# Turning the residual by DMA instead of on TensorE in a two-layer transformer trunk

## The chip, the cores and the metric

The kernel runs on one core of one Trainium2 chip. Its time is the device time of one execution in microseconds (us). The engines named below are TensorE (PE in the profile, with PEld for its weight loads), VectorE (DVE), ScalarE (ACT), GpSimd (POOL) and SyncE (SP); SP does no arithmetic, it issues transfers by DMA.

## The reference

What is computed is a decoder trunk of two layers on 256 positions with 2048 channels in float32. Layer 0 mixes with sliding-window attention and an mLSTM (a matrix memory), layer 1 with a "forgetting attention"; both have a SwiGLU feed-forward part of 5632 hidden channels.

```python
h = x                                              # (1, 256, 2048)
for layer in range(2):
    xn = rms_norm(h, norm_mix[layer])
    if layer == 0:
        mix = swa_mlstm_mixer(xn, ...)             # ends in "... @ w_out"
    else:
        mix = forgetting_attention_mixer(xn, ...)  # begins with "xn @ w_in", ends in "out @ w_out"
    h = h + mix
    xn = rms_norm(h, norm_ffn[layer])
    h = h + (silu(xn @ w_gate[layer]) * (xn @ w_up[layer])) @ w_down[layer]
return rms_norm(h, norm_final)
```

## The kernel before

**Products.** Every float32 product is made of three matmuls: operands are split into a high part and a remainder (`hi`, `lo`), and `hi·hi + hi·lo + lo·hi` is summed in PSUM. TensorE needs the left operand with the channel on the partitions, so the kernel keeps the normalised residual turned, as `xh` and `xl`, 16 tiles of 128 channels by 256 positions each. The output of a mixer stands turned in `mh`, `ml`. The 1/rms of each position is applied later, to results; the turned values carry only the norm's gain `gT`.

**Weights.** `load_raw` (L108) loads a chunk of 256 rows and 512 columns, 512 KB, on SP's queue; `split_chunk` (L151) casts it to `hi` on ACT (L154) and subtracts on DVE for `lo` (L155). There are four raw buffers and six pairs of `hi`/`lo`. `gemm` (L168) walks such chunks: 12 matmuls with 512 columns for a chunk (two tiles of channels, two of positions, three matmuls each; L182 to L184).

**Mixed pairs.** Gate and up, the two halves of a down projection, and query and key are multiplied together in `pair_group` (L431). Most pairs of tiles are done plainly (12 matmuls a matrix, L367 to L369); two or three of six or eight are "mixed": a scheme of seven products instead of eight, for which sums of the weights (L462 to L468) and sums of the turned operand are needed (`sums_of`, L217). Which pairs are mixed, and in which order pairs come, is in tables of (kind, pair), with kind 1 for mixed: `ORDER` (L36) for gate and up, `DOWN` (L37) and `DOWN_END` (L41) for the down projections. A group ends with additions on DVE that put the shared products together (L488 to L491) and into `h` (L612, then `add_out`, L259).

**Turning the residual.** `h` stands with positions on the partitions, 128 by 2 by 2048. It is made in blocks of 512 columns, and three times in the kernel all four blocks are finished and have to be turned for what follows: after each layer's output projection (for the FFN) and after layer 0's last down projection (for layer 1). These are the twelve norm blocks. `split_scaled` (L228) does one of them:

```python
pt = pm.tile([P, 2, NT, P], F32, tag="pm", name="pt")
...
nc.tensor.transpose(pt[:, i, t, :], h[:, t, k * P : (k + 1) * P], ident)      # L234
...
nc.scalar.mul(xh[:, k, :], src, g)                                            # L239
nc.vector.scalar_tensor_tensor(out=xl[:, k, :], ...)                          # L240
```

That is eight float32 transposes of 128 by 128 on TensorE for a block, then four products on ACT and four on DVE, and the sums for mixed pairs. In `out_proj` (L351) the output projection is done in two pairs of blocks: both blocks of a pair are multiplied up to the last four tiles of channels, then each one's rest is done and it is added and turned. `close` (L573) calls `add_out` and `split_scaled` at the end of layer 0's last down groups.

**A turn by DMA is in the kernel already.** The FFN's hidden values `c`, also blocks of 512 columns, are turned under the next group's matmuls: two copies on ACT separate the upper and lower 16 bits of each float (L543), four transposing DMAs on SP's queue turn these planes (L545), and two copies on ACT (L550) join them again. The joining is put off by `todo` lists of (position, function): `run_due` (L163) runs a function when `pair_group` reaches that position, behind the latest weight cast. `MID` (6) and `MID_DOWN` (5) are its positions. Twenty blocks are turned this way; the last group before each down projection is turned on TensorE.

**The start of layer 1.** After the FFN, `project` makes the last 272 columns of the input projection first (256 of the values and 16 forget gates, L969), then the gates are worked out on ACT and DVE, while `v_part(0)` makes the first 512 value columns (`first`, L1011 and L1026).

**Order.** Tiles and pools decide who waits for whom; a scheduler orders each engine's instructions when the kernel is built, and `issue_after` keeps an instruction behind another in that order. Each engine then works through its own queue in order.

## Time and profile before

| | us |
|---|---|
| median of three runs | 2113.64 |
| the runs | 2113.04 to 2115.53 |
| the profiled execution | 2115.51 |
| its span in the profile | 2113.8 |
| TensorE busy | 2096.8 (99%) |
| DVE busy | 1823.7 (86%) |
| ACT busy | 1280.7 (61%) |
| granted clock of TensorE, mean | 0.997 |

One execution is profiled, and its rows are in microseconds from the start of the span, or in nanoseconds for a mean duration. A group of instructions is named by line, engine, operation and by output and inputs (`pt<-ident,h`). "DMA to landing" is the time from the issue of a transfer to its last byte. Matmuls overlap: the next begins before the one ahead has ended, so that the cost of one is read from the distance of starts, not from its duration.

### The profile page before, as it was taken

The numbers are of one execution on the slowest core, as the hardware profiler recorded it, in microseconds if no ns is written. First come the engines' busy times: TensorE is split into PE (matmuls) and PEld (weight loads), VectorE is DVE, ScalarE is ACT, GpSimd is POOL, SyncE is SP. The second block draws the span as 40 slices with busy tenths as digits, with TensorE's granted clock in tenths as the row PEclk, the third lists the DMA queues.
The fourth block names the chain that finished last, engine by engine and source line by source line (L and its number), as shares of the span: only waits on it lengthen the run. The fifth ranks groups of instructions, "written<-read, shape, count | busy, mean of one in ns | idle before, by whom it ended". The sixth has DMA issues, their size and how long they took to land.

```text
span 2113.8 us, 26987 instructions
## 1 busy us (share of the span) xinstructions
PE 2096.8 (99%) x9654; PEld 1740.8 (82%) x9654; DVE 1823.7 (86%) x2402; ACT 1280.7 (61%) x1637; POOL 50.6 (2%) x74
## 2 busy tenths in 40 slices
PE   8999999999999999999999999999999999999998
PEld 6878888888888888888888888888888888888886
DVE  6688777899999998999887888778899998998995
ACT  6565555665577646766565546566755677556763
POOL 2100000000000000000000000000000000000000
PEclk9999999999999999999999999999999999999999
DMA  9445666766577666666675655666656667656763
GB/s 316 125 139 181 222 208 182 220 194 204 194 221 221 213 197 212 221 219 189 179 220 172 179 172 166 202 198 203 212 183 220 218 209 205 224 189 209 229 208 131
DMA packets 258998, 423.04 MB, mean 200 GB/s; under 512 B 56576, under 2 KB 64816, under 8 KB 258864
## 3 DMA queue, kind: packets, MB, share of 16 engines
q1 hardware_dynamic: 256976, 415.49, 63.0%
q0 software_dynamic: 1744, 5.81, 1.0%
...
q14 instruction: 59, 0.48, 0.1%
...
HBM read 408.67 MB, written 2.11 MB: 194 GB/s over the span
## 4 chain that ended last, share of the span: by engine, by line
PE 96%; DVE 2%; DMA 1%; issue 0%; ACT 0%; SPq 0%; DVEq 0%; POOLq 0%; POOL 0%; ACTq 0%
PE acc L367 20%; PE acc L368 20%; PE acc L369 20%; PE prod L367 5%; PE prod L368 5%; PE prod L369 5%; PE acc L184 5%; PE acc L183 5%; PE acc L182 5%; PE vacc L182 1%; PE vacc L184 1%; PE vacc L183 1%; DVE lo L155 1%; PE ptm L268 1%; PE po L338 1%
## 5 line engine op out<-in xcount | busy, mean ns | idle before, releaser
L154 ACT CAST hi<-raw 128x1024 fp32r<-128x1024 f32 (+1 forms) x664 | 676.9, 1031 | 486.9 <-PE acc L369 266.1
L155 DVE TENSOR_TENSOR lo<-raw,hi 128x1024 fp32r<-128x1024 f32 (+1 forms) x664 | 788.0, 1200 | 140.1 <-ACT hi L154 138.1
L368 PE MATMUL acc<-lo,xh 128*128 128x512 f32 x1207 | 470.2, 390 | 0.5 <-DVE lo L155 0.5
L367 PE MATMUL acc<-hi,xh 128*128 128x512 f32 x1207 | 466.6, 390 | 0.3 <-DVE u L488 0.2
L369 PE MATMUL acc<-hi,xl 128*128 128x512 f32 x1207 | 464.9, 389 | 0.0
L367 PEld LDWEIGHTS acc<-hi,xh 128*128 128x128 f32 x1207 | 226.6, 188 | 48.3 <-DVE u L488 1.1
L368 PEld LDWEIGHTS acc<-lo,xh 128*128 128x128 f32 x1207 | 226.6, 188 | 47.7 <-DVE lo L155 0.8
L369 PEld LDWEIGHTS acc<-hi,xl 128*128 128x128 f32 x1207 | 226.6, 188 | 47.2
L368 PE MATMUL acc<-lo,mh 128*128 128x512 f32 x444 | 173.1, 390 | 0.0
L369 PE MATMUL acc<-hi,ml 128*128 128x512 f32 x444 | 171.1, 389 | 0.0
L367 PE MATMUL acc<-hi,mh 128*128 128x512 f32 x444 | 170.1, 389 | 0.0
L256 ACT CAST ht<-raw 128x1024 fp32r<-128x1024 f32 x94 | 98.7, 1050 | 53.7 <-issue 19.4
L257 DVE TENSOR_TENSOR lt<-raw,ht 128x1024 fp32r<-128x1024 f32 x94 | 114.8, 1221 | 15.2 <-ACT ht L256 14.9
L182 PE MATMUL acc<-hi,mh 128*128 128x512 f32 x320 | 126.9, 397 | 0.0
L183 PE MATMUL acc<-lo,mh 128*128 128x512 f32 x320 | 125.4, 392 | 0.0
L184 PE MATMUL acc<-hi,ml 128*128 128x512 f32 x320 | 124.8, 393 | 0.0
L256 ACT CAST ht<-t 128x1024 fp32r<-128x1024 f32 x94 | 98.9, 1052 | 41.1 <-PE prod L369 28.3
L257 DVE TENSOR_TENSOR lt<-t,ht 128x1024 fp32r<-128x1024 f32 x94 | 114.6, 1219 | 7.4 <-ACT ht L256 7.4
L256 ACT CAST hi<-raw 128x512 fp32r<-128x512 f32 (+1 forms) x115 | 72.5, 630 | 79.8 <-PE acc L369 68.4
L257 DVE TENSOR_TENSOR lo<-raw,hi 128x512 fp32r<-128x512 f32 (+1 forms) x115 | 80.6, 701 | 24.6 <-ACT hi L256 24.5
L367 PEld LDWEIGHTS acc<-hi,mh 128*128 128x128 f32 x444 | 83.3, 188 | 17.5
L369 PEld LDWEIGHTS acc<-hi,ml 128*128 128x128 f32 x444 | 83.4, 188 | 17.3
...
## 6 DMA issues: line engine op xcount, KB each, us to landing
raw<-in_w_gate_dram SPq DMA_DIRECT2D x176, 512.0 KB, 4.5
raw<-in_w_up_dram SPq DMA_DIRECT2D x176, 512.0 KB, 4.7
raw<-in_w_down_dram SPq DMA_DIRECT2D x176, 512.0 KB, 4.8
raw<-in_w_in_odd_dram SPq DMA_DIRECT2D x88, 512.0 KB, 4.6
raw<-in_w_in_even_dram SPq DMA_DIRECT2D x64, 512.0 KB, 4.6
raw<-in_w_out_even_dram SPq DMA_DIRECT2D x32, 512.0 KB, 4.1
raw<-in_w_out_odd_dram SPq DMA_DIRECT2D x32, 512.0 KB, 4.4
...
```

The costliest lines, as they stand in the source:

```text
L154: latest[0] = nc.scalar.copy(hi[:, :, 0:n], raw[:, :, 0:n])
L155: nc.vector.tensor_tensor(out=lo[:, :, 0:n], in0=raw[:, :, 0:n], in1=hi[:, :, 0:n].bitcast(F32), op=ALU.subtract)
L182: nc.tensor.matmul(o, ah[:, ts], hi, start=(k == 0), stop=False)
L183: nc.tensor.matmul(o, ah[:, ts], lo, start=False, stop=False)
L184: nc.tensor.matmul(o, al[:, ts], hi, start=False, stop=(k == k_all - 1))
L256: nc.scalar.copy(dst_h, src)
L257: nc.vector.tensor_tensor(out=dst_l, in0=src, in1=dst_h.bitcast(F32), op=ALU.subtract)
L268: nc.tensor.transpose(pt[:, i, :], s_, ident)
L338: nc.tensor.matmul(po, v_of(j, 0), t0[:, j, :], start=True, stop=False)
L367: nc.tensor.matmul(o, ah, hi, start=start, stop=False)
L368: nc.tensor.matmul(o, ah, lo, start=False, stop=False)
L369: nc.tensor.matmul(o, al, hi, start=False, stop=stop)
```

## The change

All twelve norm blocks are turned by DMA. `turn_scaled` takes the place of `split_scaled`. It makes two copies on ACT that separate `h` into 16-bit planes and returns two functions: `start` issues four transposing DMAs on SP, and `join` makes two joining copies and the products and sums as before, reading SBUF instead of PSUM. Blocks 1 and 3 (n = 0 and 2) use the tiles of `c` and `tmp` as planes; blocks 2 and 4 (n = 1 and 3) use three buffers of the FFN's ring of raw chunks (`turn_tiles`).

The functions are kept in lists and run between later work. In `out_proj` the first two blocks' functions run between the chunks of blocks 3 and 4 (`run_next`), and for this the second pair of blocks is multiplied singly, first all of block 3, then all of block 4. What is left runs in the first FFN group at the positions `TURN_AT`. For layer 0's last down projection, the functions of blocks 1 and 2 run in the second group at `TURN_DOWN`, those of blocks 3 and 4 in `first_values`, the new start of layer 1: value columns on channel tiles 0 to 7, the 272-wide tail on tiles 0 to 7, then values on tiles 8 to 11, the rest of the values and the rest of the tail. `ORDER` and `DOWN_END` change: for gate and up pair 4 is mixed in place of pair 3, and the pairs now come in the order of their numbers; in `DOWN_END` the mixed pair 4 comes behind the plain pair 5.

```diff
--- before.py
+++ after.py
@@ -33,15 +33,17 @@
 OFF_QM, OFF_KM, OFF_VM, OFF_OM = 1536, 2048, 2560, 3584
 CAP = 15.0
 FILL = 24
-ORDER = ((0, 0), (0, 1), (1, 2), (0, 4), (1, 3), (0, 5), (1, 6), (0, 7))
+ORDER = ((0, 0), (0, 1), (1, 2), (0, 3), (1, 4), (0, 5), (1, 6), (0, 7))
 DOWN = {
     6: ((0, 0), (0, 1), (1, 2), (0, 3), (1, 4), (0, 5)),
     8: ((0, 0), (0, 1), (1, 2), (0, 3), (1, 4), (0, 5), (1, 6), (0, 7)),
 }
-DOWN_END = ((0, 0), (0, 1), (1, 2), (0, 3), (1, 4), (0, 5), (0, 6), (0, 7))
+DOWN_END = ((0, 0), (0, 1), (1, 2), (0, 3), (0, 5), (1, 4), (0, 6), (0, 7))
 QK_ORDER = ((0, 0), (0, 1), (1, 2), (0, 4), (1, 3), (0, 5), (1, 6), (0, 7))
 V_AT = 8
 HEAD_STEPS = ((0, 1), (0, 2), (1, 3), (0, 2), (1, 3), (2,), (3,))
+TURN_AT = (1, 2, 3, 5)
+TURN_DOWN = (2, 3, 4, 6)
 MID = 6
 MID_DOWN = 5
 RAWS = 4
@@ -225,32 +227,45 @@
         nc.vector.tensor_tensor(out=s[:, 3, :], in0=full[:, 1, 0, :], in1=s[:, 1, :], op=ALU.subtract)
         split_plain(sh, sl, s)
 
-    def split_scaled(idx, n, extra=None):
-        for half in range(2):
-            pt = pm.tile([P, 2, NT, P], F32, tag="pm", name="pt")
-            for i in range(2):
-                k = 4 * n + 2 * half + i
-                for t in range(NT):
-                    nc.tensor.transpose(pt[:, i, t, :], h[:, t, k * P : (k + 1) * P], ident)
-            for i in range(2):
-                k = 4 * n + 2 * half + i
-                src = pt[:, i, :, :].rearrange("p t q -> p (t q)")
+    def turn_scaled(room, idx, n, extra=None):
+
+        hu = h[:, :, n * NB : (n + 1) * NB].bitcast(U16).rearrange("p t (n b) -> p t n b", b=2)
+        flat, turned, ct = room.turn_tiles(n % 2)
+        for b in range(2):
+            nc.scalar.copy(flat[:, b, :, :], hu[:, :, :, b])
+
+        def start():
+            with tc.issue_after(load[0].ins):
+                for b in range(2):
+                    for t in range(NT):
+                        nc.sync.dma_start_transpose(turned[b][:, :, t, :], flat[:, b, t, :])
+
+        def join():
+            cb = ct.bitcast(U16).rearrange("p (n b) -> p n b", b=2)
+            for b in range(2):
+                nc.scalar.copy(cb[:, :, b], turned[b].rearrange("p k t q -> p (k t q)"))
+            cols = ct.rearrange("p (k q) -> p k q", k=4)
+            for i in range(4):
+                k = 4 * n + i
                 g = gT[:, idx * KT + k : idx * KT + k + 1]
-                nc.scalar.mul(xh[:, k, :], src, g)
+                nc.scalar.mul(xh[:, k, :], cols[:, i, :], g)
                 nc.vector.scalar_tensor_tensor(
-                    out=xl[:, k, :], in0=src, scalar=g, in1=xh[:, k, :].bitcast(F32), op0=ALU.mult, op1=ALU.subtract
+                    out=xl[:, k, :], in0=cols[:, i, :], scalar=g, in1=xh[:, k, :].bitcast(F32), op0=ALU.mult, op1=ALU.subtract
                 )
-            pair = 2 * n + half
-            if extra is not None and pair in mixed_of(ORDER):
-                sh, sl, pool = extra
-                j = mixed_of(ORDER).index(pair)
-
-                def copies(full):
+            for half in range(2):
+                pair = 2 * n + half
+                if extra is None or pair not in mixed_of(ORDER):
+                    continue
+                m = mixed_of(ORDER).index(pair)
+
+                def copies(full, half=half, pair=pair):
                     for i in range(2):
                         g = gT[:, idx * KT + 2 * pair + i : idx * KT + 2 * pair + i + 1]
-                        nc.scalar.mul(full[:, i, :], pt[:, i, :, :].rearrange("p t q -> p (t q)"), g)
-
-                sums_of(pool, sh[:, j, :, :], sl[:, j, :, :], copies)
+                        nc.scalar.mul(full[:, i, :], cols[:, 2 * half + i, :], g)
+
+                sums_of(room, extra[0][:, m, :, :], extra[1][:, m, :, :], copies)
+
+        return start, join
 
     def split_plain(dst_h, dst_l, src):
         nc.scalar.copy(dst_h, src)
@@ -348,20 +363,32 @@
             ks = slice(k_tile + q, k_tile + q + 2)
             split_plain(mh[:, ks, :], ml[:, ks, :], po)
 
-    def out_proj(w, idx, key, extra, begun=None):
+    def run_next(pending):
+        if pending:
+            with tc.issue_after(latest[0].ins):
+                pending.pop(0)()
+
+    def out_proj(w, idx, key, extra, room, begun=None):
         last = KT - 4
+        pending = []
         for n0 in (0, 2):
             if n0 == 0 and begun:
                 accs = begun
             else:
                 accs = [new_acc() for _ in range(2)]
-                for i in range(2):
-                    gemm(accs[i], m_of, w, (n0 + i) * NB, NB, 0, last, KT)
             for i in range(2):
+                if n0:
+                    for k0 in range(0, last, 4):
+                        gemm(accs[i], m_of, w, (n0 + i) * NB, NB, k0, k0 + 4, KT)
+                        if k0 or i == 0:
+                            run_next(pending)
                 gemm(accs[i], m_of, w, (n0 + i) * NB, NB, last, KT, KT)
                 add_out(accs[i], n0 + i)
-                split_scaled(idx, n0 + i, extra)
+                pending += turn_scaled(room, idx, n0 + i, extra)
                 square_sum(key, n0 + i)
+            if n0 == 0:
+                pending = pending[0::2] + pending[1::2]
+        return pending
 
     def three(o, ah, al, hi, lo, start, stop):
         nc.tensor.matmul(o, ah, hi, start=start, stop=False)
@@ -396,6 +423,23 @@
 
         def tmp(self, shape, name):
             return self.pool.tile(shape, F32, tag="tmp", name=name, bufs=2)
+
+        def turn_tiles(self, odd):
+            shape = [P, 4, NT, P]
+            if odd:
+                a, b, ct = (self.pool.tile([P, 2 * NB], F32, tag="raw", name="turn", bufs=self.raws) for _ in range(3))
+                flat = a.bitcast(U16).rearrange("p (b t n) -> p b t n", b=2, t=NT)
+                turned = [
+                    b.bitcast(U16)[:, i * 2 * NB : (i + 1) * 2 * NB].rearrange("p (k t q) -> p k t q", k=4, t=NT)
+                    for i in range(2)
+                ]
+                return flat, turned, ct
+            c = self.c()
+            flat = (
+                c[:, 2:4, :].bitcast(U16).rearrange("p a n -> p (a n)").rearrange("p (b t n) -> p b t n", b=2, t=NT)
+            )
+            turned = [self.pool.tile(shape, U16, tag="tmp", name="turned", bufs=2) for _ in range(2)]
+            return flat, turned, c[:, 0:2, :].rearrange("p a n -> p (a n)")
 
     class Inside(Room):
 
@@ -491,9 +535,8 @@
         nc.vector.tensor_tensor(out=c[:, 3, :], in0=prods[1], in1=c[:, 1, :], op=ALU.add)
         return plain, c
 
-    def ffn(layer, fp, sx, sd, key, idx_next=None, key_next=None, finish=None):
+    def ffn(layer, fp, room, pending, sx, sd, key, idx_next=None, key_next=None, finish=None, then=None):
         r = rstd(key)
-        room = Room(fp)
 
         def sums_x(pair):
             j = mixed_of(ORDER).index(pair)
@@ -503,7 +546,8 @@
             end = g1 == PARTS[-1]
             nk = 4 * (g1 - g0)
             order = DOWN[nk // 2]
-            todo = []
+            todo = list(zip(TURN_AT, pending))
+            pending = []
             for g in range(g0, g1):
                 par = (g1 - 1 - g) % 2
                 plain, c = pair_group(
@@ -577,7 +621,7 @@
                     finish(acc, n, gf)
                 else:
                     add_out(acc, n)
-                    split_scaled(idx_next, n)
+                    pending.extend(turn_scaled(room, idx_next, n))
                     square_sum(key_next, n)
 
             gf = None
@@ -596,9 +640,10 @@
                     sums_d,
                     [(wd, n0 * NB), (wd, (n0 + 1) * NB)],
                     DOWN_END if end and n0 == 2 else order,
-                    todo,
+                    todo + list(zip(TURN_DOWN, pending[0::2] + pending[1::2])),
                 )
                 todo = []
+                pending = []
                 if end and idx_next is None:
                     gf = [fp.tile([P, CK, NB], F32, tag="raw", name="gf", bufs=RAWS) for _ in range(2)]
                     for i in range(2):
@@ -612,13 +657,16 @@
                         nc.vector.tensor_tensor(out=o, in0=c[:, 2 * m + t, :], in1=o, op=ALU.add)
                 for m in range(2):
                     close(plain[m], n0 + m)
+        if then:
+            then(pending[0::2] + pending[1::2])
 
     def close_layer(layer, w_out, idx, key, begun=None, **rest):
         with tc.tile_pool(name=f"fp{layer}", bufs=2) as fp:
             nd = max(len(mixed_of(o)) for o in DOWN.values())
             sd = [fp.tile([P, nd, 4, P], F32R, name=f"sd{i}", bufs=1) for i in range(2)]
-            out_proj(w_out, idx, key, (*sx, Room(fp)), begun)
-            ffn(layer, fp, sx, sd, key, **rest)
+            room = Room(fp)
+            pending = out_proj(w_out, idx, key, sx, room, begun)
+            ffn(layer, fp, room, pending, sx, sd, key, **rest)
 
 
     def free_halves():
@@ -952,11 +1000,23 @@
 
     late = ctx.enter_context(tc.tile_pool(name="late", bufs=1))
     sx = [late.tile([P, len(mixed_of(ORDER)), 4, P], F32R, name=f"sx{i}") for i in range(2)]
-    close_layer(0, w_out_even[0], 2, "f0", begun=begun0, idx_next=1, key_next="m1")
-
+    wi1 = w_in_odd[0]
+    VT = 2 * FD
+    c_v = 2 * FOX_H * FD
+    vacc0 = [bank(1, "vacc") for _ in range(NT)]
+    tacc1 = new_acc()
+    FIRST_ODD = [(0, 0, NB, k) for k in range(0, 8, 2)] + [(1, 14 * FD, VT + FOX_H, k) for k in range(0, 8, 2)]
+    FIRST_ODD += [(0, 0, NB, k) for k in (8, 10)]
+
+    def first_values(pending):
+        for acc, c0, n, k0 in FIRST_ODD:
+            gemm((vacc0, tacc1)[acc], x_of, wi1, c_v + c0, n, k0, k0 + 2, KT)
+            if (acc, k0) in ((0, 4), (0, 6), (1, 4), (0, 10)):
+                run_next(pending)
+
+    close_layer(0, w_out_even[0], 2, "f0", begun=begun0, idx_next=1, key_next="m1", then=first_values)
 
     r1 = rstd("m1")
-    wi1 = w_in_odd[0]
     with tc.tile_pool(name="od", bufs=1) as od:
         def nat1(acc, n, name, bufs=1):
             t_ = od.tile([P, NT, n], F32, tag=name, name=name, bufs=bufs)
@@ -964,9 +1024,10 @@
                 nc.scalar.mul(t_[:, t, :], acc[t][:, 0:n], r1[:, t : t + 1])
             return t_
 
-        VT = 2 * FD
-        c_v = 2 * FOX_H * FD
-        acc = project(wi1, c_v + 14 * FD, VT + FOX_H)
+        gemm(vacc0, x_of, wi1, c_v, NB, 12, KT, KT)
+        vns = {0: nat1(vacc0, NB, "vn", bufs=2)}
+        acc = tacc1
+        gemm(acc, x_of, wi1, c_v + 14 * FD, VT + FOX_H, 8, KT, KT)
         fg = od.tile([P, NT, FOX_H], F32, name="fg")
         for t in range(NT):
             nc.vector.scalar_tensor_tensor(
@@ -994,8 +1055,6 @@
             j = mixed.index(pair)
             return sx[0][:, j, :, :], sx[1][:, j, :, :]
 
-        vns = {}
-
         def v_part(i):
             vw = NB if i < 3 else VT
             acc = [bank(1, "vacc") for _ in range(NT)]
@@ -1007,8 +1066,6 @@
 
             return part
 
-        first = v_part(0)
-        first(0, 8)
         pc = pm.tile([P, NB], F32, tag="pm", name="pcf")
         nc.tensor.matmul(pc[:, 0:FOX_H], upper, nl[:, 0, :], start=True, stop=True)
         nc.tensor.matmul(pc[:, FOX_H : 2 * FOX_H], ones, nl[:, 0, :], start=True, stop=False)
@@ -1023,7 +1080,6 @@
         nc.vector.tensor_copy(negct, pr[0:FOX_H, 0:S])
         scratch = dp.tile([FOX_H, S], F32, name="scratch")
         nc.gpsimd.dma_start(scratch, negct)
-        first(8, KT)
         for i in range(4):
             qt = od.tile([P, 4, S], F32, tag="qt", name="qtf")
             kt = od.tile([P, 4, S], F32, tag="kt", name="ktf")
```

## The prediction

> **What bounds the kernel now.** I read the page first, then the transposes that the change removes, TensorE's instructions around one of them, and the turns by DMA that the kernel already makes.
>
> ```profile
> span 2113.8 us, 26987 instructions
> PE 2096.8 (99%) x9654; PEld 1740.8 (82%) x9654; DVE 1823.7 (86%) x2402; ACT 1280.7 (61%) x1637; POOL 50.6 (2%) x74
> PE 96%; DVE 2%; DMA 1%; issue 0%; ACT 0%; SPq 0%; DVEq 0%; POOLq 0%; POOL 0%; ACTq 0%
> ```
>
> The third line is the chain that ended last: 96% of the span is TensorE following itself. An instruction taken off TensorE shortens the span by its own slot, as long as whatever replaces it delivers before TensorE asks. DVE at 86% has some slack and ACT at 61% much.
>
> The tile view of `pt`, the PSUM tile of the transposes:
>
> ```profile
> L234 PE MATMUL pt<-ident,h x96: 270/272/273, 296.4 to 1421.6; 128*128 128x128 f32 x96
> L239 ACT ACTIVATE xh<-pt,gT x48: 456/474/502, 300.6 to 1423.0; 128x256 fp32r<-128x256 f32 x48
> L240 DVE SCALAR_TENSOR_TENSOR xl<-pt,gT,xh x48: 474/478/484, 301.1 to 1423.5; 128x256 fp32r<-128x256 f32 x48
> ```
>
> There are 96, eight for each of twelve blocks. Their 272 ns is latency; the slot is read from starts, in TensorE's timeline:
>
> ```profile
> 295.29 0.39 PE L184 MATMUL acc<-hi,ml 128*128 128x512 f32 x1
> ...
> 296.19 0.39 PE L182 MATMUL acc<-hi,mh 128*128 128x512 f32 x1
> 296.42 0.38 PE L234 MATMUL pt<-ident,h 128*128 128x128 f32 x2
> 296.56 0.48 PE L183 MATMUL acc<-lo,mh 128*128 128x512 f32 x1
> 296.87 0.39 PE L184 MATMUL acc<-hi,ml 128*128 128x512 f32 x1
> ...
> 298.03 0.39 PE L183 MATMUL acc<-lo,mh 128*128 128x512 f32 x1
> 298.26 0.82 PE L234 MATMUL pt<-ident,h 128*128 128x128 f32 x6
> 298.83 0.48 PE L182 MATMUL acc<-hi,mh 128*128 128x512 f32 x1
> 299.15 0.40 PE L183 MATMUL acc<-lo,mh 128*128 128x512 f32 x1
> ```
>
> From 295.29 to 296.19 four 512-wide matmuls start, 0.227 us each. From 296.19 to 296.87 lie two of these and two transposes: 0.68 - 0.45 = 0.23. From 298.03 to 299.15, two and six transposes: 1.12 - 0.45 = 0.67. So a transpose costs 0.111 us with its change-over, and a block 0.90 us.
>
> **What goes: 10.7 us.** 12 blocks x 0.90. The products `xh`, `xl` stay in number (48 and 48), read from SBUF instead of PSUM; the same two forms from SBUF at the start of the kernel show whether that costs:
>
> ```profile
> L637 ACT ACTIVATE xh<-xc,gT x16: 492/495/511, 4.2 to 19.1; 128x256 fp32r<-128x256 f32 x16
> L638 DVE SCALAR_TENSOR_TENSOR xl<-xc,gT,xh x16: 477/480/486, 4.8 to 20.0; 128x256 fp32r<-128x256 f32 x16
> ```
>
> DVE 480 against 478, ACT 495 against 474: DVE gets no new work, and its count of instructions stays the same.
>
> **What comes.** Per block: two copies on ACT that separate the 16-bit halves, four transposing DMAs on SP's queue, two copies on ACT that join the halves. The kernel makes 20 such turns of the same size already, under the FFN's matmuls:
>
> ```profile
> L543 ACT COPY c<-c x40: 1037/1043/1047, 393.1 to 2035.6; 128x1024 uint16<-128x1024 uint16 x40
> 394.21 5.25 SPq L545 DMA_TRANSPOSE turned<-c  x4
> DMA to landing us min/median/max: 2.4/2.9/6.3
> L550 ACT COPY c<-turned x40: 1339/1354/1374, 406.7 to 2043.8; 128x1024 uint16<-128x1024 uint16 x40
>   DMA turned<-c: 6.4, 5
> ```
>
> ACT pays 2 x 1.04 + 2 x 1.35 = 4.8 us a block, 57 us in twelve, beside 833 us in which it is idle. SP is held 5.25 us by four issues; no weight load leaves it then. From the first copy to the last landing: 2.1 + 3 x 1.31 + 2.9 = 8.9 us, and 2.7 for the joining. The last row says that ACT waited for such landings five times in forty, 6.4 us in all. Whether stages bear it is read from windows (length, then busy time and count on PE, PEld, DVE, ACT and POOL, granted clock, DMA share, GB/s):
>
> ```profile
> 393.00:402.00 9.00, 9.00 (x42) 7.44 (x41) 7.01 (x7) 7.61 (x9) 0.00 (x0) 1.00 0.88 197
> ...
> 296.40:346.00 49.60, 49.60 (x232) 41.20 (x231) 34.07 (x48) 29.35 (x50) 0.00 (x0) 1.00 0.63 183
> 346.00:388.00 42.00, 42.00 (x191) 34.76 (x190) 37.78 (x51) 26.60 (x32) 0.69 (x1) 1.00 0.65 201
> 985.00:1027.00 42.00, 42.00 (x195) 34.78 (x194) 34.88 (x47) 24.22 (x38) 0.00 (x0) 1.00 0.43 130
> 1027.00:1045.00 18.00, 17.47 (x116) 15.88 (x115) 16.66 (x35) 11.28 (x23) 0.69 (x1) 1.00 0.65 206
> ```
>
> The first row holds a turn of today, with TensorE busy throughout. The others are the stages that get turns: the end of the first out-projection, the first FFN group, the last down group of layer 0, the start of layer 1. ACT is idle 20.2, 15.4, 17.8 and 6.7 us there and needs at most 4 x 4.8 = 19.2 over the first two. DVE is the fuller engine (37.78 of 42) and is not charged. The DMA share leaves room.
>
> **Where cover is thin.** I walked the queues in the order in which the changed kernel's instructions are built, with a matmul at 0.227 us and the durations above, and compared when each turned block can be there with when TensorE asks. ACT's queue is the one to watch: casts of weights stand behind each joining copy, which waits for its landing. SP is second: loads stand behind transposes that wait for ACT.
>
> Blocks 1 and 2 of an out-projection (edits: split in start and join, run between chunks) are needed one full block pair later, 2 x 96 x 0.227 = 43.6 us; free. Block 3, finished 21.8 us earlier than its pair mate now that the two run singly, is joined before the FFN starts; the single run itself costs nothing, since no weight is shared between blocks. Block 4 ends with the FFN's start: h added and split 3 us in, four issues until 8, landed by 11, joined and multiplied by 16 (the DMA row's median; 2.7 + 4 x 0.47). Behind it on ACT stands the last cast of the first mixed pair, done by 17; TensorE's 82nd matmul asks for it at 82 x 0.227 = 18.6. Its own pairs, 6 and 7, stay last in ORDER, so the values themselves are early. Margin 1.6 us against a landing that can be 3.4 longer (6.3 - 2.9): 0 to 1.8 us, twice (both layers). I take 0.5 each, nearest the median.
>
> Blocks 1 and 2 of layer 0's last down projection: today the additions that end a group are strewn over DVE's other work, 14.2 us from the first to the end of the last.
>
> ```profile
> 987.78 0.69 DVE L488 TENSOR_TENSOR u<-prod,c 128x512 f32<-128x512 f32 x1 [1.25 <-PE prod L369]
> 989.52 0.69 DVE L489 TENSOR_TENSOR c<-prod,u 128x512 f32<-128x512 f32 x1
> 990.12 0.68 DVE L490 TENSOR_TENSOR c<-prod,u 128x512 f32<-128x512 f32 x1
> 1000.67 1.28 DVE L262 TENSOR_TENSOR h<-acc,h 128x512 f32<-128x512 f32 x2
> ```
>
> In the changed built order ten of them stand together, 10 x 0.60 = 6 us: block 1's h is there at about 4, block 2's at 6. Both are split by 8; eight issues run from 4.9 to 15.4. The loads of the second mixed pair stand behind (one also waits until a raw buffer used as a turning plane is read) and land at 22.5; TensorE asks at 26.5, since DOWN_END moved that pair one place back. Before that, ACT's splitting copies hold the casts of the first mixed pair until 9.4, asked for at 10.9. If half of today's delay stays, (14.2 - 6) / 2 = 4.1 less the margin of 1.5, 2.6 us are lost; I take 0.5, near the built order.
>
> Blocks 3 and 4 of it: today transposes and products stand directly ahead of layer 1 and TensorE waits a little there:
>
> ```profile
> 1039.80 0.28 PE L182 MATMUL acc<-hi,xh 128*128 128x272 f32 x1
> 1039.92 0.29 PE L183 MATMUL acc<-lo,xh 128*128 128x272 f32 x1
> ...
> 1041.72 0.39 PE L182 MATMUL acc<-hi,xh 128*128 128x272 f32 x1 [0.26 <-ACT xh L239]
> 1042.76 0.51 PE L184 MATMUL acc<-hi,xl 128*128 128x272 f32 x2 [0.28 <-DVE xl L240]
> ```
>
> These last two waits, 0.5 us, go. The new start of layer 1 runs 48 matmuls of values (10.9 us) and 48 of the 272-wide tail (0.125 apart by the first two rows, 6 us) on blocks 1 and 2: 16.9 us of cover. The turn needs: ACT free for the split 6 us after the group's end (its casts wait for buffers), 8.9 to the last landing, 2.7 and the first product, some 16.6 in all. Margin nil, so 0 to 3.4; I take 1.0. That the values' columns come first costs nothing by itself: the same chunks run in another order.
>
> **Sum.** -10.7 - 0.5 + (0.5 + 0.5 + 0.5 + 1.0) = -8.7 us. The profiled execution took 2115.5 us, 1.7 around its span of 2113.8, so it would become 2106.8. The median of the three runs is 2113.64, 1.9 lower: 2105.0. With all waits at zero it is 2102.4; with all at their ends (2 x 1.8 + 2.6 + 3.4 = 9.6) 2112.0.
>
> **Rivals.**
> *The cover is too thin at the layer's edge.* SP is held by pairs of turns, 2 x 5.25 = 10.5 us each, and four raw buffers hold four chunks, 4 x 12 x 0.227 = 10.9 us of matmuls. If the buffers are not full when SP stops, TensorE runs dry by a landing, 4.8 us for a w_down load,
>
> ```profile
> raw<-in_w_down_dram SPq DMA_DIRECT2D x176, 512.0 KB, 4.8
> ```
>
> in the down group and again in layer 1, besides the 1 us at the FFNs: 11.2 - 9.6 - 1 leaves 0.6 less time, 2113.0. For it: the DMA row's 6.3, and SP waiting on ACT. Against: 0.43 DMA share there, loads issued well ahead in the built order. A longer wait has a second price:
>
> ```profile
> 152.15 0.63 PE L368 MATMUL prod<-lo,xh 128*128 128x512 f32 x1
> 152.58 0.63 PE L369 MATMUL prod<-hi,xl 128*128 128x512 f32 x1
> ...
> 156.14 0.39 PE L368 MATMUL acc<-lo,xh 128*128 128x512 f32 x1
> 156.37 0.40 PE L369 MATMUL acc<-hi,xl 128*128 128x512 f32 x1
> ```
>
> After a stretch of tiny products TensorE started matmuls 0.43 apart, then 0.23 again: a dozen cost 2.4 us more. The Trainium skill (TensorE: Matmul & The Clock Gate, Part 1) puts such a slow stretch behind an idle window of about 3.4 us; by it each dry spell above that would add these 2.4, for 2117.8, and mine would add none.
>
> *Turning by DMA is dearer than by TensorE (slower).* Place: ACT's queue at the twelve joins. If each landing takes the row's longest, 3.4 more than its median, with the casts of weights behind, and stages have under 3.4 us in hand, TensorE stands 3.4 us twelve times: 40.8 - 11.2 = +29.6, 2143. It decides from 0.93 us a block. For it: the landings' spread. Against: ACT's 6.4 us in twenty turns of today with TensorE never stopped. The Trainium skill (VectorE: DVE Perf Modes, Rules for kernel authors) advises this way: TensorE for a 128x128 transpose when PSUM will do, the DMA otherwise, 390 ns against 1309. The rows agree on the longer latency (272 ns against 2.9 us for four tiles), but TensorE's slot is 0.11 us here and the DMA's time is not on the chain.
>
> *That it doesn't do what it says* can be ruled out: the built order has 96 matmuls fewer, 48 ACT copies and 48 transposing DMAs more.
>
> **Chances.** 0.2% (4.2 us) is what three runs with 2.5 us between them can tell. Forecast, below 2109.4: 0.72. Thin cover, 2109.4 to 2117.8: 0.16. Slower: 0.12. The range, 2102 to 2113.5, goes from all waits at zero over all at their ends to the thin cover's 2113.0; under 0.2 is left out, nearly all above.
>
> **What would show it.** Right: no L234, 128 transposing DMAs, TensorE busy over 99%, waits for a turned block under 1 us at the four places; the first matmul on block 3 in layer 1 the latest. Wrong: the chain of waits shows DMA landings of turned planes or weight loads behind them, several us each, at the FFN starts or around the layer's edge, or a lower granted clock there.

## The result: 3.2 us faster, where 8.7 were forecast

| | us | runs |
|---|---|---|
| before, median | 2113.84 (2111.99 to 2116.87) | 22 |
| after, median | 2110.68 (2107.78 to 2113.77) | 22 |
| ratio after to before | 0.9984, interval 0.9978 to 0.9991 | |
| profiled execution of after | 2111.74, span 2110.0 (before 2115.51, 2113.8) | 1 |

The change is a gain that the interval separates from nothing, though it is smaller than the 0.2% set beforehand as the least that three runs could tell. The time lies inside the range, on the right side, at a third of the forecast's size.

The page of the changed kernel, the same three rows as shown of before (span; busy time of each engine; the chain that ended last by engine):

```profile
span 2110.0 us, 26911 instructions
PE 2088.3 (99%) x9558; PEld 1729.4 (82%) x9558; DVE 1817.7 (86%) x2402; ACT 1326.3 (63%) x1685; POOL 51.3 (2%) x74
PE 82%; DVE 8%; DMA 4%; ACT 3%; issue 2%; SPq 0%; POOLq 0%; POOL 0%; ACTq 0%; DVEq 0%
```

TensorE has 96 instructions and 8.5 us of busy time less, and ACT 48 copies more, as built. But the span fell by 3.8 only, and TensorE's part of the chain fell from 96% to 82%, with DVE at 8 and DMA at 4. Shares of a chain are not lost time (each step of DVE in it may have cost TensorE nothing), but they say where to look: stretches of the kernel now end on DVE and on DMA which ended on TensorE before.

To find the stretches I lined up the two profiles by TensorE's instructions, leaving out the norm blocks' transposes, and took the distance between the starts of the same matmul in both. After minus before, by stage of before's clock, in us:

| stage | after - before |
|---|---|
| start to 178 | -1.7 |
| first out-projection from 293, three blocks' transposes gone | -2.8 |
| first FFN group, 345 to 388, the fourth block's gone | -0.1 |
| rest of layer 0's first two FFN parts, to 584 | +1.1 |
| to 1001 | -0.1 |
| last down group and start of layer 1, to 1089, four blocks' gone | +0.1 |
| to 1373 | -0.3 |
| second out-projection, to 1435 | -2.8 |
| layer 1's first FFN group | +2.0 |
| to 1654 | +0.9 |
| rest | -0.1 |

So the transposes' time is gained in both out-projections, gained and given back at the layer's edge, and partly lost again in the FFN's first groups. Here is that loss, as TensorE's timeline of the changed kernel shows it (start, duration, operation; in brackets the idle time before it and who ended it):

```profile
382.03 0.50 PE L395 MATMUL prod<-lt,sx 128*128 128x512 f32 x1 [0.40 <-DVE lt L272]
...
483.88 0.81 PE L573 MATMUL pf<-ident,c 128*128 128x128 f32 x6
485.48 0.50 PE L394 MATMUL prod<-hi,mh 128*128 128x512 f32 x1 [0.55 <-ACT mh L271]
...
1046.32 0.50 PE L184 MATMUL vacc<-hi,xh 128*128 128x512 f32 x1 [0.94 <-ACT xh L251]
1065.56 0.49 PE L395 MATMUL acc<-lo,xh 128*128 128x512 f32 x1 [0.71 <-DVE lo L157]
...
1453.37 0.50 PE L395 MATMUL acc<-lo,xh 128*128 128x512 f32 x1 [0.56 <-DVE lo L157]
1454.51 0.51 PE L395 MATMUL prod<-lt,sx 128*128 128x512 f32 x1 [0.40 <-DVE lt L272]
```

Many waits of half a microsecond, none of several. At the FFN's two starts (382 and 1453) TensorE waits for the lower halves of weights from DVE (`lo`, `lt`), not for a turned block and not for a load. The chain of waits of the changed kernel just ahead of 382 (start, duration, engine and output):

```profile
375.54 1.23 DVE lt L272
376.77 0.60 DVE raw L512
377.37 1.14 DVE lo L157
378.50 0.60 DVE t L506
379.11 0.60 DVE t L507
379.71 1.13 DVE lo L157
380.84 1.15 DVE lt L272
381.99 0.04 issue
382.03 0.50 PE prod L395
```

DVE works without a gap here, and between the lower halves that TensorE asks for stand `t` and `raw`: the sums of the weights of a mixed pair (L506, L507, L512). These are no new instructions (DVE has 2402 in both). They have moved. The first of them in each kernel, from DVE's timelines, before and then after:

```profile
287.97 0.69 DVE L462 TENSOR_TENSOR t<-raw 128x512 f32<-128x512 f32 x1 [2.19 <-DMA raw<-in_w_up_dram]
```

```profile
343.64 0.69 DVE L506 TENSOR_TENSOR t<-raw 128x512 f32<-128x512 f32 x1
```

The FFN's first matmul on the turned operand starts at 343.13 before and at 338.72 after. Before, the first mixed pair was begun 55 us ahead of it, under the out-projection, where DVE has room. After, it is begun 4.9 us behind it. Windows of the first 39 us of the FFN's first group in the changed kernel, with the columns as in the prediction (length, busy time and count on PE, PEld, DVE, ACT and POOL, granted clock, DMA share, GB/s):

```profile
345.10:384.00 38.90, 38.50 (x170) 31.39 (x169) 36.86 (x47) 26.25 (x32) 0.00 (x0) 1.00 0.75 238
```

DVE is busy 36.86 of 38.90 us. What was moved into this stage fills it. The experiments ask what moved it.

### The profile page after: what moved, and what is told of

It is laid out like the page before. It is cut to its first block, busy times and chain, and to the rows that moved or that the text cites. A ratio compares the mean times of both kernels' runs of the same rounds, so it can differ in the third digit from the quotient of the medians.

```text
span 2110.0 us, 26911 instructions
## 1 busy us (share of the span) xinstructions
PE 2088.3 (99%) x9558; PEld 1729.4 (82%) x9558; DVE 1817.7 (86%) x2402; ACT 1326.3 (63%) x1685; POOL 51.3 (2%) x74
## 4 chain that ended last, share of the span: by engine, by line
PE 82%; DVE 8%; DMA 4%; ACT 3%; issue 2%; SPq 0%; POOLq 0%; POOL 0%; ACTq 0%; DVEq 0%
PE acc L395 17%; PE acc L396 17%; PE acc L394 17%; PE prod L395 4%; PE prod L394 4%; PE prod L396 4%; PE acc L186 4%; PE acc L185 4%; PE acc L184 4%; DVE lo L157 3%; DMA raw<-in_w_up_dram 1%; ACT hi L156 1%; DVE lt L272 1%; PE vacc L186 1%; PE vacc L184 1%
## 5 line engine op out<-in xcount | busy, mean ns | idle before, releaser
L396 PEld LDWEIGHTS acc<-hi,xl 128*128 128x128 f32 x1207 | 226.8, 188 | 46.8
L395 PEld LDWEIGHTS acc<-lo,mh 128*128 128x128 f32 x444 | 83.4, 188 | 17.8 <-DVE lo L157 0.5
```

The costliest lines, as they stand in the source:

```text
L395: nc.tensor.matmul(o, ah, lo, start=False, stop=False)
L396: nc.tensor.matmul(o, al, hi, start=False, stop=stop)
```

## The experiments

All ratios are to runs of the kernel before on the same chip; a difference in us is of medians.

### The transposes themselves

First, what the removal is worth without any replacement. In one kernel the old code reads `h` unturned, in the other the new code does, with the joins at the same places.

```diff
-                    nc.tensor.transpose(pt[:, i, t, :], h[:, t, k * P : (k + 1) * P], ident)
...
-                nc.scalar.mul(xh[:, k, :], src, g)
+                nc.scalar.mul(xhk, cols(k), g)
```

> The kernel before with the 96 transposes of the twelve norm blocks left out: the products read the residual unturned from SBUF, nothing takes the transposes' place, and TensorE's order is otherwise that of before. It prices the removal alone. Theory A (the slots are worth what was worked out, and the changed kernel gives most of it back in waits): 12 x 0.90 = 10.7 us less, and the 0.5 us of waits at the start of layer 1 gone: 2102.6, between 2101.5 and 2104. Theory B (TensorE's slots for transposes are partly free, so that there was never so much to gain): 5 us less or under that, 2108.5 to 2111.

2102.99, ratio 0.9952 (0.9939 to 0.9964): 10.6 us less.

```diff
-        for b in range(2):
-            nc.scalar.copy(flat[:, b, :, :], hu[:, :, :, b])
...
-                        nc.sync.dma_start_transpose(turned[b][:, :, t, :], flat[:, b, t, :])
+            pass
```

> The changed kernel with the turning left out: no splitting copies, no transposing DMAs, no joining copies; products and sums read the residual unturned, but at the places where the changed kernel runs its joins. What remains is where the work is put. Theory A1 (the loss comes from the traffic: landings, loads behind transposes on SP, copies on ACT): as fast as without turning in the old places, 2102 to 2104. Theory A2 (a good part of the loss is DVE work put into the first FFN group, 36.9 of 38.9 us busy in the changed kernel): the waits of about 1 us in each first FFN group stay, 2104.5 to 2106.5. Theory B: 2108 to 2110. In the built order the FFN's own transposes stand 11 matmuls ahead of their use, as before, so their 0.8 us twice should be gone.

2102.11, 0.9944 (0.9931 to 0.9958): 11.5 us less. The forecast's 10.7 for the removal holds, and neither the new order of blocks, pairs and columns nor the late products cost anything. The missing 8 us or so are the price of turning by DMA.

Then each half of the change alone.

```diff
-                    pending.extend(turn_scaled(room, idx_next, n))
+                    split_scaled(idx_next, n)
```

> Only the eight blocks of the two output projections are turned by DMA; the four of layer 0's last down projection are turned on TensorE and layer 1 begins with the tail as before, DOWN_END as before. Theory A (loss in the first FFN groups and at the FFN's own transposes): 8 x 0.90 = 7.2 us gained, 0.8 + 1.8 given back in the first FFN groups and 0.9 twice where the FFN's own transposes stand only one matmul ahead of their use: 2113.8 - 7.2 + 4.4 = 2111.0, between 2110 and 2112. Rival C (the loss is at the layer's edge, by loads behind the turns): 2107 to 2108.5.

2110.80, 0.9986 (0.9978 to 0.9995): eight blocks give 2.8 us, and not 8 x 0.90.

```diff
-                pending += turn_scaled(room, idx, n0 + i, extra)
+                split_scaled(idx, n0 + i, extra)
```

> Only the four blocks of layer 0's last down projection are turned by DMA, with the new DOWN_END and layer 1 beginning with value columns; the output projections' blocks are turned on TensorE with ORDER as before. Theory A by the two traces: 4 x 0.90 + 0.5 = 4.1 us gained and as much given back (0.4 in the second down group, 1.1 + 0.4 where block 3 and 4 are asked for, 1.9 in the first query and key group): 2113.8, between 2113 and 2114.8. Rival D (the edge is fine and the loss is all in the FFNs): 2110.

2114.44, 1.0005 (0.9996 to 1.0013): the four blocks at the edge give nothing. TensorE's timeline of this kernel has one wait there that alone is half of what the four blocks' transposes cost:

```profile
1050.61 0.50 PE L184 MATMUL vacc<-hi,xh 128*128 128x512 f32 x1 [1.98 <-ACT xh L251]
```

### Which part of a turn is dear: the DMAs, the copies, or neither

One kernel keeps copies and buffers and leaves out the DMAs; one keeps the DMAs and buffers and leaves out copies (nobody reads the planes); one keeps the DMAs, the waits for their landing and the buffers, with copies of 8 columns.

```diff
-                        nc.sync.dma_start_transpose(turned[b][:, :, t, :], flat[:, b, t, :])
+            pass
...
-                nc.scalar.copy(cb[:, :, b], turned[b].rearrange("p k t q -> p (k t q)"))
+                nc.scalar.copy(cb[:, :, b], flat[:, b, :, :].rearrange("p t n -> p (t n)"))
```

> The changed kernel with the transposing DMAs of the twelve blocks left out: the splitting copies, the planes' buffers and the joining copies stay, and the join reads the planes unturned. ACT's work and the ring stay; SP's hold and the landings go. In the built order the FFN's own transposes stand 2 matmuls ahead of their use (0.7 us of wait, twice). Theory S (SP's hold and the landing cause the rest of the loss): 2102.1 + 1.6 = 2103.7, no waits in the first FFN groups and at the start of layer 1. Theory Q (ACT's four copies a block and the buffers they hold cause it): waits of 1 to 2 us in the first FFN groups and at layer 1 as in the changed kernel, 2108 to 2109.

2109.41, 0.9981 (0.9972 to 0.9990). With no transposing DMA at all, most of the loss is still there.

```diff
+                        nc.sync.dma_start_transpose(turned[b][:, :, t, :], hu[:, t, b * NB : (b + 1) * NB])
```

> The complement: the transposing DMAs are issued at their places, reading the residual directly, but nothing reads what they write; splitting and joining copies are left out and the products read the residual unturned, as in the kernel without turning. SP's hold and the planes' buffers stay; ACT's copies and the wait for the landing go. Theory S by SP's hold: 2106 to 2107, with loads late in the first FFN groups. Theory Q, or S by the landing alone: 2102 to 2103, as without turning.

2102.28, 0.9952 (0.9939 to 0.9966): no loss, as with no turning (2102.11). 48 transposing DMAs on SP's queue cost nothing that the interval (2.9 us each way) would show.

```diff
+            nc.scalar.copy(flat[:, b, 0, 0:8], hu[:, 0, 8 * b : 8 * b + 8])
...
+                nc.scalar.copy(cb[:, 0:8, b], turned[b].rearrange("p k t q -> p (k t q)")[:, 0:8])
+                nc.scalar.copy(cb[:, 8:16, b], flat[:, b, 0, 0:8])
```

> The changed kernel with everything of a turn but the length of its copies: splitting and joining copies on ACT take 8 columns, the transposing DMAs are issued from the residual, the join waits for the landing and the planes' buffers are held until then; products and sums read the residual unturned. In the built order the FFN's own transposes stand 2 matmuls ahead of their use, as in the kernel without the DMAs (about 0.6 us twice). Theory L (length of the copies on ACT): 2102.3 + 1.2 = 2103.5, no waits in the first FFN groups. Theory H (held buffers, or casts queued behind a join that waits for its landing): 2108 to 2110, with the waits of the changed kernel.

2112.74, 0.9993 (0.9984 to 1.0002): the loss is back, and larger, with next to no work in the copies. So neither the DMAs' issue time nor ACT's copying time is the price. What the kernels that lose at the FFN's starts have in common is that block 4's splitting copies write buffers of the raw ring, which a turn then keeps until its joining copies have been read. L112 loads a weight chunk into a raw buffer; the ring has four, and a turn of an even block (2 or 4) asks for three of them. What SP waits for there is in its wait view (waiting line, releaser: total us, times, longest), first of the kernel without DMAs between 330 and 352 us, then of the changed kernel between 314 and 356:

```profile
SPq L112 <- ACT turn L243: 10.0, 1, 10.0
```

```profile
SPq L112 <- ACT turn L246: 1.0, 1, 1.0
```

In the first, a load and all behind it stood 10.0 us until ACT's joining copies of a block had let go of a buffer. In the changed kernel this wait is only 1.0 us, and it comes at 350, when the first mixed pair is already late. So a buffer that is still in use does not explain why the first pair's loads went out late. SP's timeline of the changed kernel has them (the first two rows) directly ahead of block 4's transposes:

```profile
336.89 0.46 SPq L112 DMA_DIRECT2D raw<-in_w_gate_dram  x1
337.40 0.46 SPq L112 DMA_DIRECT2D raw<-in_w_up_dram  x1
340.94 5.12 SPq L241 DMA_TRANSPOSE turn<-turn  x4
```

Block 2's buffers were read for the last time at 319.91, and block 4's splitting copies begin at 339.87. In the 17 us before 336.89 nothing used a buffer of the ring, and seven other loads of gate and up went out. The pair's loads are late because SP's queue was built so. It fits that in the program block 4's split stands ahead of these loads and so has the first claim on the ring; how the scheduler hands buffers out was not tried by itself.

### The other suspects: order, SP's queue, ACT's late casts

The order of instructions: in the changed kernel the FFN's own transposes (`pf`) stand one matmul ahead of what reads them (483.88 above), where there were eleven before. An order edge moves them twelve ahead again.

```diff
+                        if pos == 3 and m == 1 and pin[0]:
+                            behind.enter_context(tc.issue_after(pin[0].ins))
```

> The changed kernel with one order edge added: the second matrix of plain pair 3 in the down projections stands behind the last of the FFN's own eight transposes on TensorE, so that these stand 12 matmuls ahead of the mixed pair that reads them, in place of 1. Theory P (the builder's order of these transposes costs 0.8 + 0.1 us in each layer): 2110.7 - 1.9 = 2108.8, and no wait for mh there. Rival (what is late is the hidden value itself, whatever the order): 2110.7, with the wait in front of the transposes instead.

2111.28, 0.9986 (0.9978 to 0.9995). The wait at 485 and its twin in layer 1 are gone, and the time isn't better: others came, of 0.37 at 572 and 0.29 at 2045. The next two kernels, and the one with two buffers, keep this edge (the expectations call it the pinned kernel).

SP's queue: the weights of the first FFN group are loaded from GpSimd's queue, past all transposes.

```diff
+                by[0] = nc.gpsimd if g == 0 else nc.sync
```

> The pinned kernel, and in the first gate and up group of each layer the weight loads are issued from GpSimd's queue, so that the four transposing DMAs of block 4 on SP hold no load. Theory S (the waits in the first FFN groups are loads behind the turn on SP: no load is issued for 11 us from 337.4 to 348.4 us in the changed kernel's trace): 1.2 and 1.5 us less, 2106.2, no wait over 0.2 us in these groups. Theory R (it is the ring of four raw buffers, three of which the turn holds): the same as the pinned kernel, 2108.8. Rival (loads from GpSimd are slower themselves): above 2109.

2120.84, 1.0034 (1.0022 to 1.0047): slower. From that queue the loads took longer to land, on its page (KB, then median us to landing), and the mixed pair was no earlier; so it says nothing about SP.

```profile
raw<-in_w_gate_dram POOLq DMA_DIRECT2D x16, 512.0 KB, 5.0
raw<-in_w_gate_dram SPq DMA_DIRECT2D x160, 512.0 KB, 4.4
```

The positions of the joins in the FFN, to spread ACT's work:

```diff
-TURN_AT = (1, 2, 3, 5)
+TURN_AT = (1, 3, 5, 5)
```

> The pinned kernel with TURN_AT = (1, 3, 5, 5): block 4's transposing DMAs one position later and its join two. More loads stand ahead of the turn on SP, but the join comes closer to its use. Theory S: SP no longer waits 3 us for the split with loads behind it, 0.5 to 1.5 us less than pinned, 2107.3 to 2108.3. Rival (the join becomes late for pair 6, at position 6): 2110 or more, with a wait for xh or xl at the end of the first groups.

2116.65, 1.0014 (1.0004 to 1.0023): worse. Block 4's buffers are read until 26.4 us (layer 0) and 29.3 us (layer 1) behind the FFN's start, where it is 14.1 and 15.9 in the changed kernel, and TensorE waits for what DVE adds:

```profile
386.28 0.50 PE L395 MATMUL acc<-hi,xh 128*128 128x512 f32 x1 [1.00 <-DVE u L537]
```

ACT relieved: the late blocks' copies on GpSimd, which is idle, with all twelve blocks and with the out-projections' eight.

```diff
+        copy = nc.gpsimd.tensor_copy if n == 3 or idx == 1 else nc.scalar.copy
```

> The changed kernel, but GpSimd makes the splitting and joining copies of the late blocks (block 4 of the output projections, all four of the layer's edge). ACT is relieved of 4.8 us a block; what such a copy takes on GpSimd no trace of this case shows. Theory L: if one takes under 2.5 us, the waits in the first FFN groups (0.8 and 2.0 us) and most of the edge's (4.7) go, 2105 to 2108. Rival (GpSimd's copies are so slow that the joins come late): above 2112, waits for xh at the end of the first groups and at layer 1.

2131.02, 1.0084 (1.0070 to 1.0098).

> Only the output projections' blocks turned by DMA (edge on TensorE), with GpSimd copying for block 4. Theory L with copies under 2.5 us: 2113.8 - 7.4 + 1.2 for the FFN's own transposes, 2107.6. Rival (slow copies): 2111 or more.

2124.06, 1.0045 (1.0032 to 1.0059). The tile view of `turn` in the second (min, median, max in ns; first and last start) shows the joining copy at 2.4 us in the median where ACT takes 1.36. Block 4's buffers are read until 25.3 and 28.4 us behind the FFN's start:

```profile
L247 ACT COPY turn<-turn x4: 1338/1357/1362, 314.4 to 1391.7; 128x1024 uint16<-128x1024 uint16 x4
L247 POOL COPY turn<-turn x4: 1767/2364/4269, 349.0 to 1426.8; 128x1024 uint16<-128x1024 uint16 x4
```

### The ring of raw buffers

If the ring is the cause, a turn that leaves it alone ahead of the FFN must bring the gain back. First without block 4 (which stays on TensorE, as does the edge):

```diff
+                if n0 + i < 3:
+                    pending += turn_scaled(room, idx, n0 + i, extra)
+                else:
+                    split_scaled(idx, 3, (*extra, room))
```

> Only blocks 1 to 3 of the two output projections are turned by DMA; block 4 of each, which ends as the FFN begins, and the four blocks at the layer's edge are turned on TensorE. In the built order the FFN's own transposes stand 11 and 14 matmuls ahead. Theory F (what is lost in the first FFN groups is block 4's turn alone): 6 x 0.90 = 5.4 us, all kept, 2108.3, with no wait over 0.2 us in these groups. Rival (blocks 1 to 3 cost as well, or the builder's order gives back elsewhere): 2110 to 2111.

2108.93, 0.9978 (0.9969 to 0.9987): 4.7 us less, with an interval of 2.7 to 6.6, where six blocks are worth 5.4. Nothing is lost in the FFN.

Two buffers in place of three, for all twelve blocks, by joining into the buffer of the split planes:

```diff
-                return flat, turned, ct
+                return flat, turned, a
```

> The pinned kernel, but blocks 2 and 4 join into the buffer that held the splitted planes, so that a turn holds two raw buffers and not three. Theory R (the ring): the mixed pairs' loads start earlier, 1.5 to 2.5 us less than pinned, 2106.3 to 2107.3. Theory S: no more than 0.5 less, 2108.3 to 2108.8.

2116.97, 1.0013 (1.0004 to 1.0022): no help, and the theory that the number of buffers matters (2106.3 to 2107.3) missed by 10 us. The first mixed pair still begins 4.9 us behind the FFN's start: its first load goes out 3.0 us ahead of block 4's split here too, and block 4's buffers are read until the same 14.1 us behind the FFN's start. What counts for the first pair is that block 4 uses the ring at all. Why this kernel is slower than with three buffers is not cleared up; in the last down group TensorE stood at three places and then started eight matmuls 0.43 us apart:

```profile
1011.43 0.50 PE L395 MATMUL acc<-hi,sd 128*128 128x512 f32 x1 [0.84 <-ACT hi L272]
1012.38 0.50 PE L395 MATMUL acc<-hi,mh 128*128 128x512 f32 x1 [0.45 <-ACT hi L157]
1014.46 0.63 PE L396 MATMUL acc<-lo,mh 128*128 128x512 f32 x1 [1.00 <-DVE lo L158]
```

Then, on top of the six blocks, the first two of the edge by DMA as well:

```diff
+                    if n < 2:
+                        pending.extend(turn_scaled(room, idx_next, n))
+                    else:
+                        split_scaled(idx_next, n)
```

> Blocks 1 to 3 of the output projections as in the kernel with six blocks, and blocks 1 and 2 of layer 0's last down projection by DMA too, with the new DOWN_END; blocks 3 and 4 there on TensorE. By the stage ledger of the changed kernel these two gain 1.75 us and give 0.9 back: 2108.9 - 0.85 = 2108.1. Rival (the builder's order or ACT's copies give back all): 2109 or more.

2110.18, 0.9985 (0.9976 to 0.9994): two blocks more, and no faster than six. TensorE's timeline has the loss at the layer's edge:

```profile
1031.97 0.88 PE L276 MATMUL pt<-ident,h 128*128 128x128 f32 x6 [1.18 <-DVE h L304]
1039.73 0.52 PE L186 MATMUL acc<-hi,xl 128*128 128x272 f32 x2 [1.71 <-DVE xl L282]
```

At last the out-projections' eight blocks with block 4 off the ring: its planes go into the tiles `c` and `tmp`, as those of blocks 1 and 3 do, and, since block 3 has these, block 3 is joined ahead of block 4's split.

```diff
-        flat, turned, ct = room.turn_tiles(n % 2)
+        flat, turned, ct = room.turn_tiles(n == 1)
...
+                while n0 + i == 3 and pending:
+                    run_next(pending)
```

> All eight blocks of the output projections turned by DMA with copies of full length, edge on TensorE; but block 4's planes lie in the tiles of c and tmp, which block 3 has left, and not in the ring of raw buffers. Block 3's join runs ahead of block 4's split for this. Theory H (held raw buffers stop SP's loads): no wait over 0.2 us in the first FFN groups, 8 x 0.92 = 7.4 us kept, 2106.5 to 2107.5, against 2110.8 for the same kernel on the ring. Rival (the join's place in ACT's queue, whatever it holds): 2110 to 2111, with the waits of 0.6 to 0.8 us at the end of the first groups.

2103.78 (2102.35 to 2104.53), 0.9953 (0.9939 to 0.9966): 9.7 us less than before, and 6.9 less than the change as made, better than the 2106.5 to 2107.5 forecast for it. It differs from the kernel with 2110.80 in these lines alone. Its page:

```profile
span 2101.8 us, 26925 instructions
PE 2085.1 (99%) x9590; PEld 1732.3 (82%) x9590; DVE 1821.6 (87%) x2402; ACT 1311.7 (62%) x1669; POOL 52.9 (3%) x74
PE 97%; DVE 1%; DMA 0%; issue 0%; ACT 0%; SPq 0%; DVEq 0%; POOLq 0%; POOL 0%; ACTq 0%
```

TensorE is 97% of the chain again, with DVE and ACT doing the same instructions. The mixed pair's loads go out at 311.53 and 312.08, as soon as block 2's planes are being joined. Its first sum is back under the out-projection, 19 us ahead of the FFN's start (337.55), and the second pair's too:

```profile
318.56 0.69 DVE L535 TENSOR_TENSOR t<-raw 128x512 f32<-128x512 f32 x1 [0.32 <-DMA raw<-in_w_up_dram]
...
326.73 0.68 DVE L535 TENSOR_TENSOR t<-raw 128x512 f32<-128x512 f32 x1
```

and the window of the FFN's start has, with the same 170 matmuls, 2.8 us less on DVE than that of the changed kernel (36.86):

```profile
344.00:382.00 38.00, 38.00 (x170) 31.46 (x169) 34.10 (x47) 28.38 (x35) 0.69 (x1) 1.00 0.76 233
```

The edit bundles three things: block 4 off the ring, block 3 joined earlier, and a built order that has the FFN's own transposes 14 matmuls ahead. The kernel with the order edge alone shows that the last does not do it. In the kernel with six blocks the lead is back without the earlier join, though block 4's turn, copies and all, is absent there. Within this edit the first two weren't parted.

The same edit with all twelve blocks:

```diff
+        flat, turned, ct = room.turn_tiles(n == 1 or n == 3 and idx == 1)
```

> The changed kernel, all twelve blocks by DMA, with the one edit of the kernel off the ring: block 4 of each output projection is turned in the tiles of c and tmp, and block 3's join runs ahead of its split. The edge's blocks 2 and 4 stay on the ring. Theory H with the edge as in the kernel that has only the edge by DMA (2114.4, 0.8 us above before): the first FFN groups and the FFN's own transposes wait for nothing, and the edge gives back its gain: 2103.8 + 0.8 = 2104.6, between 2103.5 and 2106. Rival (edge and output projections do not add up, since the edge's part depends on the order that the builder finds): below 2103 or above 2106.

2109.50, 0.9978 (0.9968 to 0.9988). The sum of 2104.6 missed: this is 5.7 us above the eight blocks, where the edge alone cost 0.8, so the rival holds that the two parts don't add up. In the profile the stage of the layer's edge (985 to 1089 us) gives back the edge's gain again, and in layer 1 a landing was late: four transposes issued from 1417.8 had landed at 1424.2. ACT's timeline, and TensorE's behind it:

```profile
1424.65 1.35 ACT L246 COPY c<-turned 128x1024 uint16<-128x1024 uint16 x1 [3.00 <-DMA turned<-c]
```

```profile
1431.25 0.73 PE L396 MATMUL prod<-ht,sx 128*128 128x512 f32 x2 [1.49 <-ACT ht L271]
```

This is the mechanism that the prediction feared at every join, seen once in this profile. The profiled execution took 2107.07 and is one of the faster ones, so what the median lost beyond this is not seen.

The kernels that bear on this, side by side. Lead is the time from the first sum of a mixed pair's weights to the FFN's first matmul on the turned operand; lost is what the first 320 such matmuls took beyond the 72.53 us that both kernels without turning take, less the 0.93 us of block 4's transposes where TensorE does them (in the kernel before, it is 0.99 and 0.98, transposes and all). One profile each, layer 0 and layer 1:

| kernel | lead, us | lost, us |
|---|---|---|
| before without turning | 52.6, 46.8 | 0, 0 |
| after without turning | 52.8, 46.8 | 0, 0 |
| DMAs only | 26.9, 23.8 | 0, 0 |
| edge only | 54.6, 48.8 | 0.1, 0.1 |
| six blocks | 19.0, 16.3 | 0, 0 |
| six blocks and two of the edge | 18.1, 14.9 | 0, 0 |
| eight, off the ring | 19.0, 15.2 | 0, 0.3 |
| twelve, off the ring | 19.1, 14.6 | 0, 2.5 (the landing) |
| after | -4.9, -6.7 | 0.9, 2.0 |
| out-projections only | -4.9, -7.7 | 0.8, 3.3 |
| after, order edge | -4.9, -6.8 | 0, 2.2 |
| after, no DMAs | -4.9, -4.9 | 0.9, 1.5 |
| tiny copies | -5.7, -7.7 | 1.4, 3.5 |
| after, two buffers | -4.9, -6.9 | 0, 2.0 |
| after, later start | -4.9, -7.5 | 3.0, 5.2 |
| after, copies on GpSimd | -4.9, -6.9 | 3.7, 7.4 |
| out-projections, copies on GpSimd | -5.3, -7.3 | 4.8, 8.6 |
| after, loads from GpSimd | -11.0, -12.6 | 5.4, 7.1 |

In layer 1 every kernel without a lead lost 1.5 us or more and no kernel with one lost over 0.3, but for the late landing. In layer 0 the loss is smaller, and two kernels escape it in this stretch. Of the kernels that begin as late as the changed one, those that keep block 4's buffers longer (later start, copies on GpSimd) lost more, so the time for which buffers are kept seems to count too, on top of the late first pair.

The layer's edge is another matter. Lined up with the new code without turning, the stage from 985 to 1089 us takes 4.7 us more in the changed kernel, 2.7 with tiny copies, 1.9 without the DMAs and nothing with the DMAs only (one profile each). Neither half of a turn makes this loss alone.

### One part of the difference is chance

The first 1.7 us of the stage table come before any instruction has moved (the order on TensorE is the same until 290 us). Most of it is the slow stretch near 152 that the prediction quoted: 12 matmuls at half the clock in that profile of before, 7 in that of after, and seven tiny products just ahead of them that took 2.50 us there and 1.67 here. The same program of before, profiled again:

> The kernel before, looked at once more. It has 12 matmuls at half rate after 149 us in the profile of before, the changed kernel 7, and their instructions up to 290 us stand in the same order. If the stretch is a matter of the execution, this profile has another number of them and its span moves by 0.2 us for each; if it belongs to the program, 12 again and 2113.8.

2113.52, and 7 such matmuls. Across the kernels' profiles there were 0 to 13, with the same instructions up to there. Windows of 2 us at that place, of before and of the new code without turning (the number behind the five engines is the granted clock):

```profile
151.00:153.00 2.00, 2.00 (x5) 1.53 (x5) 1.67 (x5) 0.23 (x2) 0.00 (x0) 0.50 0.00 0
```

```profile
151.00:153.00 2.00, 2.00 (x11) 1.62 (x10) 1.66 (x4) 1.90 (x5) 0.00 (x0) 1.00 0.00 0
```

It is worth up to 13 x 0.2 = 2.6 us in one execution. The profile of the eight blocks off the ring had none of it, so about 2.8 of its 12.0 us of span against before's profile are this. The medians are over several executions each (five for the eight blocks off the ring); how many of them had the stretch is not seen, nor whether some kernels have it more often than others.

## Why the prediction was partly right and where it failed

- **What goes, 10.7.** Right: 10.6 and 11.5 us without turning. So is the slot of 0.90 a block: the alignment gives 0.92 to 0.93.
- **ACT and SP have room.** Right: with the DMAs alone nothing was lost, and copies of 8 columns gained nothing. Block 4's turn itself ran as sketched or sooner: in layer 0 landed 8.6 us behind the FFN's start and multiplied by 14.1, where 11 and 16 were worked out.
- **"DVE gets no new work", so it "is not charged".** This is the step that failed. The count was right, but I took DVE's load in each stage from the profile of before as if it stayed there. Its window of 42.0 us at the first FFN group had 37.78 busy already; the mixed pairs' sums that came in from the out-projection had no room. DVE became the engine that TensorE waits for there, and its share of the whole chain rose from 2% to 8%. The prediction's signs of being right mostly came all the same (128 transposing DMAs; the longest wait for a turned block 0.94 us, at block 3 in layer 1): none was set on `lo` and `lt`, where the FFN's loss sat. That the time still lies inside the range is luck: its slow end was made of waits for landings and loads, and other waits came.
- **Who else wants the raw buffers.** The prediction followed ACT's and SP's queues in order, and took the ring into account only at the last down group ("one also waits until a raw buffer used as a turning plane is read"). At the out-projections the even blocks use a ring whose other user is the loading of the FFN's first mixed pairs. With block 4 in the ring these loads stand in SP's queue directly ahead of its transposes, though no instruction used the ring from 319.91 to 336.89, and the lead fell from 55 us to less than nothing.
- **FFN starts, 0.5 each.** Sized for the landing alone. Out-projections alone: forecast -7.2 + 1.0 = -6.2, measured -2.8, so 4.4 us lost for 1.0. With the ring free the same eight blocks measured -9.7 (interval -12.9 to -7.2): all of their 7.2, and the chance above may be in the rest. So the ring accounts for the out-projections' loss within the interval; the step had no term for it. About as much again was lost at the edge.
- **Order on TensorE.** I read the built order at four places, all at the norm blocks. It had moved the FFN's own transposes as well, from eleven matmuls ahead to one: 0.8 us in each layer, though taking that away alone gained nothing. TensorE's two rows in before, to be read against 483.88 and 485.48 above:

```profile
486.07 0.82 PE L529 MATMUL pf<-ident,c 128*128 128x128 f32 x6
...
489.23 0.39 PE L367 MATMUL prod<-hi,mh 128*128 128x512 f32 x1
```

- **The layer's edge, 0.5 + 1.0.** Mis-sized: four blocks' 3.6 and the 0.5 of today's waits were expected back less 1.5; the four alone measured +0.8 (interval -0.8 to +2.7), 3.4 worse. The rival "the cover is too thin at the layer's edge" had the place right, but neither the size (9.6) nor the form: 3.6 + 0.5 + 0.8 = 4.9 were given back, in many small waits (the longest 1.98 us, in the kernel with the edge alone) and not in two dry spells. One step of it was added up wrong: as written, 6 + 8.9 + 2.7 and 0.5 for the first product are 18.1 us and not 16.6, so that the cover of 16.9 us was 1.2 short by the prediction's own terms. In the last down group the mixed pairs' first sums moved from 980.57 and 997.73 to 992.48 and 1009.29, and between 984.38 and 1001.53 SP issued eight transposes and no load. Which of this makes the loss at the edge stays open: DVE's additions, which the waits at 1031.97 and 1039.73 name, the thin cover and the ring are all possible, and the stage's 4.7, 2.7, 1.9 and 0 us above suggest that copies, buffers and landings each have a part.
- **The dear landing.** The tile view of `turn` in the changed kernel has the spread that the prediction took from the row of today's turns:

```profile
DMA to landing us min/median/max: 2.4/2.5/6.3
```

It cost TensorE once, in the profile of twelve blocks off the ring. As a rule for all twelve (the slower rival) it is refuted.
